# A decoder block with a mixture of experts on one core: where the gate2 rows are made, how the row of final_g comes in, and how the last scaling is cut

## The chip, the cores and the metric

The kernel runs on one NeuronCore of one Trainium2 chip, written in Bass and Tile: engines PE (matrix products), PEld (its weight loads), DVE (vector), ACT (scalar), POOL (GpSimd) and SP, which here only issues DMAs. Tile makes the semaphores and, unless a stretch of the program is marked as ordered by hand, the order of the instructions on each engine. The metric is the device time of one execution in microseconds (us).

## The reference, cut to what matters

One decoder layer on 256 tokens of 1024 numbers (float32): a mixing half (two kinds of attention, gates, output projection) and a channel half. A conditioning vector `c` gives six rows of 1024 numbers, `mod = silu(c) @ ada_w + ada_b`; the last of them is `gate2`. The half that this change touches:

```python
h2 = rmsnorm(x, norm2_g[l]) * (1.0 + scale2) + shift2
y = hierarchical_moe(h2, ...)   # top-1 of 4 groups, then top-2 of its 4 experts, SwiGLU
x = x + gate2 * y
...
return rmsnorm(x, final_g)      # x * rsqrt(mean(x*x) + eps) * final_g
```

## The kernel before

Tokens lie on partitions in two tiles of 128 (`t` = 0, 1); the 1024 columns are cut in two halves of 512 (`n` = 0, 1).

**The gate2 rows.** `adaacc[5, j]` holds, for half `j` of gate2, partial sums that lie over the partitions. `mod_rows(5)` multiplies them on PE with a square of ones, which sums over partitions and leaves the same row on all 128 of them (L477, tile `bc`, one product of 128x512 in float32, which runs as two passes each), and ACT copies the result back (L486, `adarow`). The rows are read much later, by DVE, when it weighs the down products (`weigh`, L1323). Before, `mod_rows(5)` is called in pair 0 of the experts.

**The router** (from about L1020 to L1112; order by hand on PE, DVE and ACT). The token logits lead to `rt_selb` (which experts each token takes), then PE counts positions (`rk`, L1085 to L1087), DVE makes `pos` and the one-hot tiles, and PE gathers tokens by expert (`hg`, L1212). Between these steps PE waits for DVE. In two of the waits PE does products whose result nobody reads, `keep_clock(3)` and `keep_clock(4)` (L171, tile `warm`, bf16 128x512).

**The experts.** Sixteen experts go in eight pairs `p`, two experts side by side on the 128 columns of PE's array. SP issues the loads of their weights in order through a ring of buffers: gate and up of pair `p` (`g`, `u`, L206), down of pair `p-1` (`d`, L206); for the last pair the down weights come in six pieces (L1242). PE's order is written by hand: gate products, up products (L1252), the slot weights (`st`, L1262 and L1264), the transposes of the activations (`actT`, L1286), down products (`dps`, L1309; L1297 in the last pair), and the scatter back to tokens that adds into `oacc` in PSUM (L1343), which already holds `x`. DVE weighs a down product (`yt`), ACT casts it to a high part (`yh`), DVE makes the low part (`yl`, L1330, L1335).

**The end.** `final_row` takes final_g, loaded as 8 rows of 128 numbers (`fgrow`), and spreads it on all partitions by eight small products on PE (L1138, 8 rows of the array each, two passes each) and two ACT copies (L1141, tile `fg`). It stands behind the last down products of pair 6. The columns of the last pair come in three parts (`PARTS`: 512, 256, 256). `norm_part` squares a part on ACT, with its sum per token into `ss` (L1155), and multiplies it on DVE with `fg` (L1158); `norm_end` adds the last sums (L1170), POOL takes the power −1/2 of both token tiles at once (L1171), then ACT and DVE scale (L1174, L1175, L1177), and per token tile ACT's queue issues one output transfer (L1178) and SP's another (L1179). An overflow branch behind it (more than 64 tokens for one expert) is not taken here.

Of the kernel before, what the change touches and what calls it, by code (L numbers as in the profile page):

```python
# [8 lines left out]
F32 = mybir.dt.float32  # L9
# [4 lines left out]
ALU = mybir.AluOpType  # L14
# [3 lines left out]
P = 128  # L18
D = 1024
T = 256  # L20
NT = T // P
KD = D // P
# [39 lines left out]
def hybrid_block_kernel(  # L62
# [23 lines left out]
    nc = tc.nc  # L86
    V, S, G, PE = nc.vector, nc.scalar, nc.gpsimd, nc.tensor

    x = x[0]
    out = out[0]  # L90
# [13 lines left out]
    def psa(name):  # L104
        return ps_a.tile([P, 512], F32, name=name, tag="psa")
# [61 lines left out]
    def keep_clock(n):  # L167

        ps = psa("warm").rearrange("p (b s) -> p b s", b=4)
        for _ in range(n):  # L170
            PE.matmul(ps, identb, identb.unsqueeze(1).broadcast_to([P, 4, P]), start=True, stop=True)  # L171
# [37 lines left out]
    st = Stream()  # L209
# [259 lines left out]
            V.tensor_tensor(lo, adaacc[which, j], hi.bitcast(F32), op=ALU.subtract)  # L469
            msplit[which].append((hi, lo))  # L470

    def mod_rows(which):

        for j in range(2):
            ps = psa(f"bc{which}{j}")
            if which == 5:
                PE.matmul(ps, ones, adaacc[which, j], start=True, stop=True)  # L477
            else:
                for i, part in enumerate(msplit[which][j]):
                    PE.matmul(ps, selr if (which, j) in ON_PE else onesr, part, start=(i == 0),  # L480
                              stop=(i == 1))
            if which == 4:
                V.scalar_tensor_tensor(adaacc[4, j], ps, 1.0, norm2[0][:, 512 * j:512 * j + 512],
                                       op0=ALU.add, op1=ALU.mult)
            else:
                S.copy(adaacc[which, j], ps)  # L486
# [567 lines left out]
    h2_hi(1, 1)  # L1054
    seed(1, 1)
    weigh_logits(1)
    keep_clock(3)

    larger = moe.tile([P, SETS, 16], F32, name="larger", bufs=1)
    G.memset(larger, 0.0)  # L1060
# [25 lines left out]
    PE.matmul(rk[:, NE:2 * NE], onesb, selv[:, 0, :], start=True, stop=False)  # L1086
    PE.matmul(rk[:, NE:2 * NE], strictb, selv[:, 1, :], start=False, stop=True)  # L1087
    h2_lo(0, 1)
    keep_clock(4)

    pos = keep.tile([P, NT, NE], F32, name="pos")
    V.scalar_tensor_tensor(pos, rk[:, 0:2 * NE].rearrange("p (t e) -> p t e", t=NT), 1.0, selv,
# [32 lines left out]


    PARTS = [slice(0, 512), slice(512, 768), slice(768, 1024)]
    fgrow = small.tile([P, P], F32, name="fgrow", tag="lgs")[0:KD, :]
    nc.scalar.dma_start(fgrow, final_g.rearrange("(k p) -> k p", p=P))
    fg = []  # L1130

    def final_row():

        fg.append(st.tile("fg")[:, 0:D])
        for n in range(2):
            ps = psa(f"fg{n}")
            for k in range(4):
                PE.matmul(ps[:, k * P:(k + 1) * P],  # L1138
                          ident[0:KD, 4 * n + k:4 * n + k + 1].broadcast_to([KD, P]), fgrow,
                          start=(k == 0), stop=True, skip_group_check=True)  # L1140
            S.copy(fg[0][:, 512 * n:512 * n + 512], ps)  # L1141

    norm = {}

    def norm_part(i):

        c = PARTS[i]
        n, cs = c.start // FW, slice(c.start % FW, c.start % FW + c.stop - c.start)
        if i == 0:
            norm["o"] = late.tile([P, NT, D], F32, name="o", tag="s8", bufs=2)  # L1150
            norm["ss"] = small.tile([P, len(PARTS), NT], F32, name="ssf", tag="ssf")
        o, ss = norm["o"], norm["ss"]
        for t in range(NT):
            junk = act[:, 0:c.stop - c.start]
            S.activation(junk, oacc[t][n][:, cs], AF.Square, scale=D ** -0.5,  # L1155
                         accum_out=ss[:, i, t:t + 1])
            if c is not PARTS[-1]:
                V.tensor_tensor(o[:, t, c], oacc[t][n][:, cs], fg[0][:, c], op=ALU.mult)  # L1158
        if c is not PARTS[-1]:

            if i == 0:
                V.tensor_scalar(ss[:, 0, :], ss[:, 0, :], EPS, None, op0=ALU.add)
            else:
                V.tensor_tensor(ss[:, i, :], ss[:, i, :], ss[:, i - 1, :], op=ALU.add)

    def norm_end():
        o, ss = norm["o"], norm["ss"]
        c, cs = PARTS[-1], slice(PARTS[-1].start - FW, FW)
        r = small.tile([P, NT], F32, name="rstdf", tag="rstd")
        V.tensor_tensor(r, ss[:, len(PARTS) - 1, :], ss[:, len(PARTS) - 2, :], op=ALU.add)  # L1170
        G.tensor_tensor(r, r, mhalf, op=ALU.pow)  # L1171
        for t in range(NT):
            rt_ = r[:, t:t + 1]
            S.mul(o[:, t, 0:512], o[:, t, 0:512], rt_)  # L1174
            V.scalar_tensor_tensor(o[:, t, c], oacc[t][1][:, cs], rt_, fg[0][:, c], op0=ALU.mult,  # L1175
                                   op1=ALU.mult)
            V.tensor_scalar(o[:, t, 512:c.start], o[:, t, 512:c.start], rt_, None, op0=ALU.mult)  # L1177
            nc.scalar.dma_start(out[t * P:(t + 1) * P, 0:512], o[:, t, 0:512])  # L1178
            nc.sync.dma_start(out[t * P:(t + 1) * P, 512:], o[:, t, 512:])  # L1179

    st.cycle = [ring2] * 3 + [ring] * 6 + ring1 * 3 + [ring2] + [ring3] * 2 + [ring2] * 2 + [ring]
# [174 lines left out]
    with tc.manual_schedule(engines={PE.engine}):  # L1356
        gather(0, 0)
        gather(0, 1)
        for p in range(NP):
# [15 lines left out]
            silu_up(p)  # L1375
            slot_weights(p)
            if p == 0:
                mod_rows(5)
                nmaxi = most_tokens()
                act_transpose(p)  # L1380
            else:
                down_rows(p - 1, 0)
                act_transpose(p)
                down_rows(p - 1, 1)
# [2 lines left out]
                gather((p + 1) // 2, 1)  # L1387
        p = NP - 1
        load_down(p)
        final_row()  # L1390
        scatter_pair(p - 1, 0, whole_cols[0])
        weigh_low(p - 1, 1)
        down(p, 0, PARTS[0])
# [10 lines left out]
        scatter_pair(p, 1, PARTS[2])  # L1404
        norm_part(2)

    norm_end()


    nmaxv = nc.values_load(nmaxi[0:1, 0:1], min_val=0, max_val=T)  # L1410
# [96 lines left out]
```

## Time and profile before

| | us |
|---|---|
| runs shown | 468.78, 470.38, 470.97 (median 470.38) |
| profiled execution | 470.29, its span 468.6 |
| busy in the span: PE, DVE, ACT, POOL | 448.2, 220.6, 160.6, 14.7 |
| bytes moved | 158.46 MB, 338 GB/s on the mean |
| mean granted clock of PE | 0.989 |

A busy engine need not be the bound: PE and the DMA engines are both nearly always busy while the experts run. What tells is which of them waits for the other, so the rows further down are taken from the stretches in which the change lies: the router, pair 0, the end of pair 6, and the tail.

### The profile page before, as it was taken

Reading aid. Unit: us, or ns where it says so; the run is one execution under the profiler, and the core shown is the slowest. Engines: PE = TensorE matmul, PEld = TensorE weight load, DVE = VectorE, ACT = ScalarE, POOL = GpSimd, SP = SyncE. Lnnn points to the kernel's source line nnn. Section 1 sums busy time; section 2 is a strip of 40 time slices with the busy share of each in tenths; the row PEclk is TensorE's granted clock in tenths of the full one; section 3 lists DMA queues with packets and bytes.
Section 4 is the critical chain, followed back from the end, with each engine's and each line's share of the span. In section 5 each row is a group of like instructions: output and inputs, shape, how many; then the busy total and the mean of one; then the engine's idle time right before and its main releaser. Section 6 shows DMA issues by size and latency. Waiting matters only on the chain. (4 is left out here: it accounts for less than half of the span.)

```text
span 468.6 us, 6867 instructions
## 1 busy us (share of the span) xinstructions
PE 448.2 (96%) x2724; PEld 281.2 (60%) x2724; DVE 220.6 (47%) x378; ACT 160.6 (34%) x292; POOL 14.7 (3%) x51
## 2 busy tenths in 40 slices
PE   5999999999999999999899999999999999999991
PEld 1769988976889999978453345333533335333440
DVE  5558878956999964787640030031202111020332
ACT  3543686465663444363641012011201102110222
POOL 5210000000000000000100000000000000000000
PEclk9999999999999999999999999999999999999986
DMA  8999978789797979976779999999999999999502
GB/s 290 368 324 354 295 267 287 247 287 382 254 374 255 385 263 407 422 308 219 294 258 408 424 420 418 422 419 421 420 421 419 422 419 421 420 420 404 196 0 94
DMA packets 51971, 158.46 MB, mean 338 GB/s; under 512 B 6448, under 2 KB 16728, under 8 KB 40160
## 3 DMA queue, kind: packets, MB, share of 16 engines
q1 hardware_dynamic: 51568, 157.44, 87.6%
q8 instruction: 23, 0.38, 0.3%
q10 hardware_dynamic: 368, 0.55, 0.3%
q14 instruction: 12, 0.10, 0.1%
HBM read 156.93 MB, written 1.05 MB: 337 GB/s over the span
## 5 line engine op out<-in xcount | busy, mean ns | idle before, releaser
L1252 PE MATMUL gps<-g,hg 128*64 128x512 f32 x256 | 57.9, 596 | 0.0
L1252 PE MATMUL ups<-u,hg 128*64 128x512 f32 x256 | 56.6, 595 | 0.0
L1309 PE MATMUL dps<-d,aT 128*64 128x512 f32 x224 | 51.2, 598 | 0.0
L1281 DVE TENSOR_TENSOR act<-act,ups 128x512 f32<-128x512 f32 x8 | 5.5, 687 | 93.6 <-PE ups L1252 93.6
L409 PE MATMUL g_acc<-hT,wsp 128*128 128x256 f32 x384 | 48.4, 285 | 0.3 <-DVE wsp L363 0.3
L409 PEld LDWEIGHTS g_acc<-hT,wsp 128*128 128x128 f32 x384 | 46.7, 191 | 1.6 <-issue 1.0
L1252 PEld LDWEIGHTS ups<-u,hg 128*64 128x64 f32 x256 | 17.9, 137 | 35.3 <-issue 35.3
L1252 PEld LDWEIGHTS gps<-g,hg 128*64 128x64 f32 x256 | 17.4, 137 | 33.2 <-issue 32.6
L1309 PEld LDWEIGHTS dps<-d,aT 128*64 128x64 f32 x224 | 14.8, 136 | 25.4 <-issue 25.2
L446 DVE SCALAR_TENSOR_TENSOR adarow<-adaw,cact,adarow 128x512 f32<-128x512 f32 x40 | 29.6, 743 | 0.4
L1327 ACT CAST yh<-yt 128x512 fp32r<-128x512 f32 x15 | 9.3, 618 | 56.7 <-DVE yt L1323 56.7
L1267 ACT CAST sT<-st 128x256 fp32r<-128x256 f32 x8 | 3.0, 372 | 63.4 <-PE st L1264 63.4
L940 PE MATMUL wo<-wsp,mT 128*128 128x512 f32 x96 | 23.7, 400 | 0.7 <-DVE wsp L363 0.7
L878 PE MATMUL br<-oT,wsp 128*128 128x256 f32 x192 | 23.2, 282 | 0.0
L1280 ACT ACTIVATE act<-gps 128x512 f32<-128x512 f32 x8 | 4.8, 598 | 53.7 <-PE gps L1252 53.7
L878 PEld LDWEIGHTS br<-oT,wsp 128*128 128x128 f32 x192 | 23.0, 188 | 0.2 <-DVE wsp L363 0.2
L1335 DVE TENSOR_TENSOR yl<-yt,yh 128x512 fp32r<-128x512 f32 x7 | 4.8, 692 | 34.3 <-PE oacc L1343 32.4
L940 PEld LDWEIGHTS wo<-wsp,mT 128*128 128x128 f32 x96 | 17.6, 188 | 5.2 <-DVE wsp L363 1.1
L1323 DVE SCALAR_TENSOR_TENSOR yt<-dps,ws,adarow 128x512 f32<-128x512 f32 (+1 forms) x17 | 12.2, 719 | 14.3 <-PE dps L1309 8.3
L1288 DVE COPY aT<-actT 128x512 f32<-128x512 f32 x8 | 5.5, 691 | 27.0 <-PE actT L1286 27.0
L1212 PEld LDWEIGHTS hg<-onehot,h2s 128*128 128x128 f32 x128 | 15.7, 191 | 4.2 <-ACT yh L1327 2.4
L1212 PE MATMUL hg<-onehot,h2s 128*128 128x256 f32 x128 | 16.8, 287 | 1.0 <-DVE h2s L1012 0.5
(295 smaller groups left out, 679.4 us busy)
## 6 DMA issues: line engine op xcount, KB each, us to landing
g<-in_expert_w_gate SPq DMA_DIRECT2D x32, 1024.0 KB, 14.6
u<-in_expert_w_up SPq DMA_DIRECT2D x32, 1024.0 KB, 16.3
d<-in_expert_w_down SPq DMA_DIRECT2D x30, 1024.0 KB, 17.2
adaw<-in_ada_w SPq DMA_DIRECT2D x16, 1024.0 KB, 6.4
ada<-in_ada_w SPq DMA_DIRECT2D x8, 512.0 KB, 8.9
ada<-in_ada_w SPq DMA_DIRECT2D x16, 256.0 KB, 8.5
wo<-in_w_out SPq DMA_DIRECT2D x4, 1024.0 KB, 12.9
kaw<-in_w_in SPq DMA_DIRECT2D x4, 512.0 KB, 6.6
```

What stands on the lines that cost most here:

```text
L409: PE.matmul(self.acc[m // 2][:, (m % 2) * T:(m % 2 + 1) * T], w[a][:, kk, m * P:(m + 1) * P], hT[b][:, k, :], start=(k == 0 and i == 0 and ...
L446: V.scalar_tensor_tensor(acc, adaw[which, j, k // 4][:, k % 4, :], cact[:, k:k + 1], acc, op0=ALU.mult, op1=ALU.add)
L878: PE.matmul(bacc[br][m // 2][:, (m % 2) * T:(m % 2 + 1) * T], wk[a][:, 0, m * P:(m + 1) * P], oT[br][b][:, k, :], start=(k == 0 and i == 0 ...
L940: PE.matmul(acc[t][n], mT[b][:, k, t * P:(t + 1) * P], ws[k // 2][a][:, k % 2, :], start=(k == 0 and i == 0), stop=(k == KD - 1 and i == 2))
L1212: PE.matmul(ps[:, kk * T:(kk + 1) * T], h2s[t][i][:, k * P:(k + 1) * P], oh[:, t].rearrange("p e s -> p (e s)"), start=(n == 0 and kk == 0 ...
L1252: PE.matmul(ps[64 * i:64 * i + 64, :], hg[:, k, (lo + i) * CAP:(lo + i + 1) * CAP], wt[nm, p][half][i][:, k % 4, :], start=(k == 0), stop= ...
L1280: S.activation(av, in_place(gu["g", p]), AF.Silu)
L1281: V.tensor_tensor(av, av, in_place(gu["u", p]), op=ALU.mult)
L1288: V.tensor_copy(aT, ap.rearrange("p (f s) -> p f s", f=KF))
L1309: PE.matmul(ys[p, FW * n][64 * i:64 * i + 64, :], aTs[p][:, 2 * h + k, 64 * i:64 * i + 64], dt_[p, h][i][:, k, FW * n:FW * n + FW], start= ...
L1323: V.scalar_tensor_tensor(y, ps, ws, adaacc[5, n][:, cs], op0=ALU.mult, op1=ALU.mult)
L1327: S.copy(hi, y)
```

## The change

It does four things. The gate2 rows are made one half at a time, each in the place of a `keep_clock`, in the router, and leave pair 0. `final_row` goes with its load and its ACT copies; a DMA on SP's queue, behind the last down weights, spreads final_g on all partitions. The last sum and the power are taken per token tile, in an order written by hand for DVE, ACT and POOL. And tile 0's first output transfer goes to SP's queue instead of ACT's.

```diff
@@ -469,9 +469,9 @@
             V.tensor_tensor(lo, adaacc[which, j], hi.bitcast(F32), op=ALU.subtract)
             msplit[which].append((hi, lo))
 
-    def mod_rows(which):
-
-        for j in range(2):
+    def mod_rows(which, js=(0, 1)):
+
+        for j in js:
             ps = psa(f"bc{which}{j}")
             if which == 5:
                 PE.matmul(ps, ones, adaacc[which, j], start=True, stop=True)
@@ -1054,7 +1054,7 @@
     h2_hi(1, 1)
     seed(1, 1)
     weigh_logits(1)
-    keep_clock(3)
+    mod_rows(5, (0,))
 
     larger = moe.tile([P, SETS, 16], F32, name="larger", bufs=1)
     G.memset(larger, 0.0)
@@ -1086,7 +1086,7 @@
     PE.matmul(rk[:, NE:2 * NE], onesb, selv[:, 0, :], start=True, stop=False)
     PE.matmul(rk[:, NE:2 * NE], strictb, selv[:, 1, :], start=False, stop=True)
     h2_lo(0, 1)
-    keep_clock(4)
+    mod_rows(5, (1,))
 
     pos = keep.tile([P, NT, NE], F32, name="pos")
     V.scalar_tensor_tensor(pos, rk[:, 0:2 * NE].rearrange("p (t e) -> p t e", t=NT), 1.0, selv,
@@ -1125,21 +1125,6 @@
 
 
     PARTS = [slice(0, 512), slice(512, 768), slice(768, 1024)]
-    fgrow = small.tile([P, P], F32, name="fgrow", tag="lgs")[0:KD, :]
-    nc.scalar.dma_start(fgrow, final_g.rearrange("(k p) -> k p", p=P))
-    fg = []
-
-    def final_row():
-
-        fg.append(st.tile("fg")[:, 0:D])
-        for n in range(2):
-            ps = psa(f"fg{n}")
-            for k in range(4):
-                PE.matmul(ps[:, k * P:(k + 1) * P],
-                          ident[0:KD, 4 * n + k:4 * n + k + 1].broadcast_to([KD, P]), fgrow,
-                          start=(k == 0), stop=True, skip_group_check=True)
-            S.copy(fg[0][:, 512 * n:512 * n + 512], ps)
-
     norm = {}
 
     def norm_part(i):
@@ -1155,7 +1140,7 @@
             S.activation(junk, oacc[t][n][:, cs], AF.Square, scale=D ** -0.5,
                          accum_out=ss[:, i, t:t + 1])
             if c is not PARTS[-1]:
-                V.tensor_tensor(o[:, t, c], oacc[t][n][:, cs], fg[0][:, c], op=ALU.mult)
+                V.tensor_tensor(o[:, t, c], oacc[t][n][:, cs], fg[:, c], op=ALU.mult)
         if c is not PARTS[-1]:
 
             if i == 0:
@@ -1166,16 +1151,20 @@
     def norm_end():
         o, ss = norm["o"], norm["ss"]
         c, cs = PARTS[-1], slice(PARTS[-1].start - FW, FW)
-        r = small.tile([P, NT], F32, name="rstdf", tag="rstd")
-        V.tensor_tensor(r, ss[:, len(PARTS) - 1, :], ss[:, len(PARTS) - 2, :], op=ALU.add)
-        G.tensor_tensor(r, r, mhalf, op=ALU.pow)
+        rs = small.tile([P, NT], F32, name="rstdf", tag="rstd")
+        last = len(PARTS) - 1
         for t in range(NT):
-            rt_ = r[:, t:t + 1]
-            S.mul(o[:, t, 0:512], o[:, t, 0:512], rt_)
-            V.scalar_tensor_tensor(o[:, t, c], oacc[t][1][:, cs], rt_, fg[0][:, c], op0=ALU.mult,
+            V.tensor_tensor(rs[:, t:t + 1], ss[:, last, t:t + 1], ss[:, last - 1, t:t + 1],
+                            op=ALU.add)
+        for t in range(NT):
+            G.tensor_tensor(rs[:, t:t + 1], rs[:, t:t + 1], mhalf[:, 0:1], op=ALU.pow)
+        for t in range(NT):
+            r = rs[:, t:t + 1]
+            S.mul(o[:, t, 0:512], o[:, t, 0:512], r)
+            V.scalar_tensor_tensor(o[:, t, c], oacc[t][1][:, cs], r, fg[:, c], op0=ALU.mult,
                                    op1=ALU.mult)
-            V.tensor_scalar(o[:, t, 512:c.start], o[:, t, 512:c.start], rt_, None, op0=ALU.mult)
-            nc.scalar.dma_start(out[t * P:(t + 1) * P, 0:512], o[:, t, 0:512])
+            V.tensor_scalar(o[:, t, 512:c.start], o[:, t, 512:c.start], r, None, op0=ALU.mult)
+            (nc.sync, nc.scalar)[t].dma_start(out[t * P:(t + 1) * P, 0:512], o[:, t, 0:512])
             nc.sync.dma_start(out[t * P:(t + 1) * P, 512:], o[:, t, 512:])
 
     st.cycle = [ring2] * 3 + [ring] * 6 + ring1 * 3 + [ring2] + [ring3] * 2 + [ring2] * 2 + [ring]
@@ -1375,7 +1364,6 @@
             silu_up(p)
             slot_weights(p)
             if p == 0:
-                mod_rows(5)
                 nmaxi = most_tokens()
                 act_transpose(p)
             else:
@@ -1387,7 +1375,8 @@
                 gather((p + 1) // 2, 1)
         p = NP - 1
         load_down(p)
-        final_row()
+        fg = st.tile("fg")[:, 0:D]
+        nc.sync.dma_start(fg, final_g.unsqueeze(0).broadcast_to([P, D]))
         scatter_pair(p - 1, 0, whole_cols[0])
         weigh_low(p - 1, 1)
         down(p, 0, PARTS[0])
@@ -1404,7 +1393,8 @@
         scatter_pair(p, 1, PARTS[2])
         norm_part(2)
 
-    norm_end()
+    with tc.manual_schedule(engines={V.engine, S.engine, G.engine}):
+        norm_end()
 
 
     nmaxv = nc.values_load(nmaxi[0:1, 0:1], min_val=0, max_val=T)
```

On PE, in the router, behind the start of the last `oacc` (`bc` is the product that spreads a gate2 row, `rk` the position count):

```order
 L986 MATMUL oacc_2583<-xs,ident 128x512
-L171 LDWEIGHTS identb
-L171 MATMUL warm<-identb 128x512
-L171 LDWEIGHTS identb
-L171 MATMUL warm<-identb 128x512
-L171 LDWEIGHTS identb
-L171 MATMUL warm<-identb 128x512
+L477 MATMUL bc_2586<-adarow_1597,onesr 128x512
 L1085 LDWEIGHTS strictb
 L1085 MATMUL rk<-rt_selb,strictb 128x16
```

The three unread products have gone and one `bc` stands there; the other one stands in the same way behind the third `rk` product, in place of the four.

On PE, in pair 0, from the slot weights to the gate products of pair 1, the kernel before has:

```order
L1262 MATMUL st_2741<-ident,onehot_2618 128x128 x2
L1264 MATMUL st_2741<-rt_comb,onehot_2618 128x16 x2
L477 MATMUL bc_2751<-adarow_1597,onesr 128x512
L477 MATMUL bc_2754<-adarow_1608,onesr 128x512
L1119 MATMUL pmT<-ident,rt_pmax 1x128
L1286 MATMUL actT_2765<-ident,act 128x128 x4
L1252 MATMUL gps_2796<-g_0_2772,hg 64x512
```

With the change, the same stretch of PE reads:

```order
L1251 MATMUL st_2736<-ident,onehot_2613 128x128 x2
L1253 MATMUL st_2736<-rt_comb,onehot_2613 128x16 x2
L1119 MATMUL pmT<-ident,rt_pmax 1x128
L1275 MATMUL actT_2754<-ident,act 128x128 x4
L1241 MATMUL gps_2785<-g_0_2761,hg 64x512
```

The two `bc` products are gone from between `st` and the transposes of `act`.

On DVE, in the tail, from the weighing of the middle part on, the kernel before has:

```order
L1323 SCALAR_TENSOR_TENSOR yt<-dps_3697,ws,adarow_1608 128x256
L1158 TENSOR_TENSOR o<-oacc_2533,fg 128x512
L1158 TENSOR_TENSOR o<-oacc_2567,fg 128x512
L1162 TENSOR_SCALAR ssf<-ssf 128x2
L1323 SCALAR_TENSOR_TENSOR yt<-dps_3718,ws,adarow_1608 128x256
L1158 TENSOR_TENSOR o<-oacc_2551,fg 128x256
L1158 TENSOR_TENSOR o<-oacc_2583,fg 128x256
L1164 TENSOR_TENSOR ssf<-ssf 128x2
L1170 TENSOR_TENSOR rstdf<-ssf 128x2
L1175 SCALAR_TENSOR_TENSOR o<-oacc_2551,rstdf,fg 128x256
L1177 TENSOR_SCALAR o<-o,rstdf 128x256
L1175 SCALAR_TENSOR_TENSOR o<-oacc_2583,rstdf,fg 128x256
```

With the change, from the same place on DVE:

```order
L1312 SCALAR_TENSOR_TENSOR yt<-dps_3675,ws,adarow_1608 128x256
L1147 TENSOR_SCALAR ssf<-ssf 128x2
L1143 TENSOR_TENSOR o<-oacc_2533,fg 128x512
L1143 TENSOR_TENSOR o<-oacc_2567,fg 128x512
L1312 SCALAR_TENSOR_TENSOR yt<-dps_3696,ws,adarow_1608 128x256
L1143 TENSOR_TENSOR o<-oacc_2551,fg 128x256
L1143 TENSOR_TENSOR o<-oacc_2583,fg 128x256
L1149 TENSOR_TENSOR ssf<-ssf 128x2
L1157 TENSOR_TENSOR rstdf<-ssf 128x1 x2
L1164 SCALAR_TENSOR_TENSOR o<-oacc_2551,rstdf,fg 128x256
L1166 TENSOR_SCALAR o<-o,rstdf 128x256
L1164 SCALAR_TENSOR_TENSOR o<-oacc_2583,rstdf,fg 128x256
```

`ssf`, the small sum that waits for the squares of both token tiles, has moved ahead of the two 512-wide products with `fg`, and one sum for both tiles has become two.

## Rows read from the trace of the kernel before

**Rows 1.** Windows: us, busy us (instructions) of PE, PEld, DVE, ACT, POOL, PEclk, DMA, GB/s.

```profile
226.00:241.00 15.00, 12.26 (x92) 7.45 (x92) 11.32 (x33) 9.06 (x15) 0.82 (x2) 1.00 0.95 360
241.00:441.00 200.00, 200.00 (x965) 79.25 (x961) 31.11 (x49) 26.80 (x62) 0.00 (x0) 1.00 0.99 407
441.00:450.00 9.00, 9.00 (x40) 4.34 (x39) 2.44 (x4) 1.80 (x4) 0.00 (x0) 0.81 0.00 0
```

**Rows 2.** Timeline of the router: start, us, engine, line, operation, [idle before, its releaser].

```profile
233.21 0.81 PE L171 MATMUL warm<-identb 128*128 128x512 bf16 x3
...
234.23 0.18 PE L1085 MATMUL rk<-rt_selb,strictb 128*128 128x16 bf16 x1 [0.20 <-DVE rt_selb L1080]
...
234.32 1.02 PE L171 MATMUL warm<-identb 128*128 128x512 bf16 x4
...
235.77 0.78 PE L1212 MATMUL hg<-onehot,h2s 128*128 128x256 f32 x3 [0.43 <-DVE onehot L1194]
...
238.03 0.59 ACT L1216 COPY hg<-hg 128x512 f32<-128x512 f32 x1 [4.04 <-PE hg L1212]
```

**Rows 3.** Timeline, PE and DVE in pair 0, behind the up products.

```profile
254.84 0.69 DVE L1281 TENSOR_TENSOR act<-act,ups 128x512 f32<-128x512 f32 x1 [13.53 <-PE ups L1252]
...
255.27 1.96 PE L477 MATMUL bc<-adarow,onesr 128*128 128x512 f32 x4
...
257.07 0.47 PEld L1286 LDWEIGHTS actT<-ident,act 128*128 128x128 f32 x4 [0.34 <-ACT adarow L486]
```

**Rows 4.** Loads of expert weights by line: count, issue times, us from issue to landing.

```profile
L206 SPq DMA_DIRECT2D d<-in_expert_w_down x28: 327/328/422, 225.8 to 410.2; - x28
...
DMA to landing us min/median/max: 7.1/15.5/19.9
...
L1242 SPq DMA_DIRECT2D d<-in_expert_w_down x6: 368/1209/9254, 412.7 to 432.1; - x6
...
DMA to landing us min/median/max: 10.5/15.4/20.4
```

**Rows 5.** Timeline, PE and DVE at the end of pair 6.

```profile
437.66 3.65 PE L1309 MATMUL dps<-d,aT 128*64 128x512 f32 x16
...
441.14 0.69 DVE L1330 TENSOR_TENSOR yl<-yt,yh 128x512 fp32r<-128x512 f32 x1 [0.74 <-ACT yh L1327]
...
441.25 2.05 PE L1138 MATMUL fg<-fgrow,ident 8*128 8x128 f32 x16
...
443.22 0.73 PE L1343 MATMUL oacc<-yh,sT 128*128 128x512 f32 x2
...
444.38 5.26 PE L1297 MATMUL dps<-d,aT 128*64 128x512 f32 x16
```

**Rows 6.** Windows behind the final_g products.

```profile
444.50:447.50 3.00, 3.00 (x8) 0.88 (x10) 0.69 (x1) 0.00 (x0) 0.00 (x0) 0.50 0.00 0
...
448.00:450.00 2.00, 2.00 (x10) 0.66 (x7) 0.30 (x1) 0.00 (x0) 0.00 (x0) 1.00 0.00 0
```

**Rows 7.** Timeline of the tail, and the one-column power of the router.

```profile
454.33 1.41 DVE L1158 TENSOR_TENSOR o<-oacc,fg 128x512 f32<-128x512 f32 x2 [1.13 <-ACT act L1155]
...
456.92 0.93 DVE L1158 TENSOR_TENSOR o<-oacc,fg 128x256 f32<-128x256 f32 x2 [0.67 <-ACT act L1155]
...
458.47 0.20 ACT L1155 ACTIVATION_READ_ACCUMULATOR act<-oacc 128x1 f32 x1
...
459.20 0.16 DVE L1170 TENSOR_TENSOR rstdf<-ssf 128x2 f32<-128x2 f32 x1 [1.29 <-ACT act L1155]
...
459.44 0.70 POOL L1171 TENSOR_TENSOR rstdf<-rstdf,mhalf 128x2 f32<-128x2 f32 x1 [230.29 <-DVE rstdf L1170]
...
460.18 1.33 ACT L1174 ACTIVATE o<-o,rstdf 128x512 f32<-128x512 f32 x2 [1.00 <-POOLq L1411]
...
460.95 1.01 SPq L1179 DMA_DIRECT2D out<-o  x2
...
L250 POOL TENSOR_TENSOR rstd<-rstd,mhalf x2: 557/559/561, 223.0 to 228.6; 128x1 f32<-128x1 f32 x2
```


## The prediction

> **What bounds the kernel now.** The sum below is made against the profiled execution: 470.29 us, of which the span is 468.6 and 1.69 lies around it. It stands 0.09 us under the median of the runs shown (470.38), so a change of its span carries over to the median as it is.
>
> I first cut the span into stretches by stage [rows 1]. From 241 to 441 us, where the eight pairs of experts run, PE is busy for 200.0 of 200 us, and the DMA engines are 0.99 busy too: two engines look like the bound at once. Which one it is, the landings tell [rows 4]. The last ordinary down load is issued by 410.2 and no load of that line took longer than 19.9 us, so it has landed by 430.1; PE first reads it in the second half of the down products at 437.66 [rows 5], 7.5 us later. The last pair's loads (issued from 412.7, at most 20.4 to landing) have their first user at 444.38: the first of them is there by 433.1, some 11 us ahead, and the second megabyte, issued one load later, still several. So PE waits for no weights; the loads run ahead by at least 7.5 us. **PE's own instruction stream sets the time from 241 to about 453 us**, and a us taken out of it is a us of the result as long as the sum of such cuts stays under 7.5. Behind it comes a tail in which ACT, DVE and POOL hand a last row of numbers on (453 to 462), and the transfer of the output.
>
> Ahead of it, in the router (226 to 241), PE is busy for 12.26 of 15 us only [rows 1]: it waits for DVE, twice with products that nobody reads (`warm`) in the wait [rows 2].
>
> **The change, part by part.**
>
> *1. The two gate2 products in the router.* They take the places of three and of four `warm` products [rows 2]. The three start at 233.21 and the next PE work, `rk`, at 234.23, when DVE has `rt_selb`. One gate2 product is two passes of the array. The two, four passes, stand from 255.27 on, and `actT`'s weight load, with one tiny product between, at 257.07 [rows 3]; so one is 0.90 us at most, and I take 0.88. It fits: 233.21 + 0.88 = 234.1, ahead of 234.23. The second starts at 234.32 and ends about 235.2; the gather starts at 235.77. I take 0 for both; the waits for DVE that end at 234.23 and 235.77 cover them. Were that cover gone the price would be at most 1.8 us (both products in full); below nothing it can't go, since DVE's work there is the same. ACT's two copies of the rows (0.58 us each) come behind the last `h2s` cast; ACT stands idle for 4.04 us ahead of its first `hg` copy at 238.03 [rows 2]. The gather's second buffer in PSUM now waits for such a copy, but both are done by about 236.1 (235.2, a handing over and 0.58), and the second buffer is wanted only when the first is full, which ACT copies at 238.03. Cost 0.
>
> *2. The same products taken out of pair 0.* There they stand on PE's stream, between `st` and `actT`. Without them PE would be 1.80 us earlier (255.27 to 257.07), but `actT` reads `act`, and DVE is not done with that before 254.84 + 0.69 = 255.53. With about 0.1 us for the handing over, `actT`'s weight load goes from 257.07 to about 255.62: **−1.45 us**. Bounds: −1.2 (a slower handing over, ACT's `sT` and `ws` copies in the way) and −1.8 (no wait).
>
> *3. The row of final_g.* PE's sixteen small products go: PE's step from 441.25 to 443.22, 1.97 us [rows 5]. What is late next is `yl`: DVE finishes it at 441.14 + 0.69 = 441.83, and PE, which then starts the scatter at 441.25, needs it two products later (0.58 us; the four from 443.22 to 444.38 took 1.16), at 441.83. I allow 0.1 us for that meeting: **−1.9 us** (bounds −1.6 and −2.0). In their place SP issues one load of 512 KB, the row on all 128 partitions, behind the last down loads (the last is issued at 432.1 [rows 4], now 1.5 us earlier). At the 407 GB/s of the stage [rows 1] it holds the engines for 1.3 us, behind all weights, so none of these is late. Its landing is bounded below by that transfer and above by the slowest landing of its queue, 20.4 us: 432 to 451, and I take 442 to 443, just behind the last weights, since the queue is then nearly empty. DVE asks for it at about 450. The two ACT copies that go (1.1 us at 443.4) were beside PE's work.
>
> *4. PE's clock.* At 1.00 from 226 to 441 [rows 1], the granted clock falls right behind the small products: 0.50, the 1.2 GHz level, from 444.5 to 447.5, and 1.00 (2.4 GHz) again from 448 on [rows 6]. What PE did before the fall is just the stretch with products of 8 rows instead of 128, the only such stretch among the experts. The sixteen down products behind it took 5.26 us; the same sixteen at full clock took 3.65 [rows 5]. Without the small products I expect no fall: **−1.6 us** (bounds 0, if it falls anyway, and −1.7).
>
> Against that stands a rule. The Trainium skill ("TensorE: Matmul & The Clock Gate", section "Why this matters for your kernels") puts a fall of the clock down to PE standing idle between bursts of matmuls. This case's trace does not bear that out: PE is busy for 9.00 of the 9 us from 441 to 450 [rows 1], and the clock fell all the same. By that rule the small products are not to blame, and term 4 would be 0, the sum 466.5.
>
> I keep −1.6, as the fall came right behind the one odd stretch.
>
> *5. The tail.* DVE now does the small sum `ssf` ahead of the two 512-wide products with `fg`, and `ssf` waits for both squares. DVE began these products at 454.33, between the squares; it will begin behind the second, some 0.85 us later in this stretch. That eats the 0.67 us in which DVE stood idle ahead of the next `o` at 456.92 [rows 7], and PE's last scatter waits for that one: **+0.1 us** to +0.3.
>
> Then the rstd by token tile. Tile 0's sum of squares is there at 458.47 + 0.20 = 458.67; add 0.16, the handing over 0.08, the power on one column 0.56 (against 0.70 on two) and 0.04 to ACT: ACT and DVE start tile 0 at 459.54 instead of 460.18. Tile 1's power comes behind on POOL, 459.50 to 460.06, in time for ACT's second product (half of 1.33 us later, at 460.2). So both engines end 0.64 us earlier. SP issues three transfers instead of two; it issued its two from 460.95 to 461.96, about 0.4 to 0.5 apart, so the third follows DVE's last product without a queue. With 0.1 for that: **−0.55 us** (bounds −0.2, if SP's three queue up, and −0.7).
>
> The fgrow load on ACT's queue goes; ACT works on past it. Nothing.
>
> Sum: −1.45 − 1.9 − 1.6 + 0.1 − 0.55 = −5.4 us, from 470.29 to **464.9 us**. PE's cuts ahead of the last weights' use are 1.45 + 1.9 = 3.35, under the 7.5 us by which the loads run ahead.
>
> **The rivals.**
>
> *The clock falls anyway* (chance 0.16). For it: one fall is all that the trace has, and what else may bring one is not in its rows. Against: 200 us of the experts at 1.00, and the one fall right behind the small products. The skill's rule above speaks for this rival. Then term 4 is missing, 466.5 us. A fall elsewhere, in the router, costs about the same.
>
> *PE does not gain, the loads are the bound after all* (0.05). For: DMA 0.99 busy from 241 to 441, and the lead of the loads shrinks towards the end. Against: 7.5 us are left. It decides if the lead is really near 0: terms 2 and 3 are then waits for weights, and 470.29 − 1.6 − 0.45 = 468.2 us stays.
>
> *The waits of the router are too short* (0.05): the change moves the products without getting them off the path, the gather starts 1.7 us later, 466.6 us.
>
> *Slower: the row of final_g lands late* (0.04). The one place where the change adds a wait for a transfer is DVE's first product with `fg`; behind it in DVE's queue stands the weighing of the last down part, and PE's last scatter and ACT's last squares wait for that. Each us past about 450 is a us of the result. It decides against the change past 450.2 + 5.4 = 455.6, that is over 24 us after an issue at about 431. For it: it is last in SP's queue, and 128 copies of one row are read. Against: no load of the last pair took over 20.4 us [rows 4]. At 458 it would give 464.9 + 7.8 = 472.7 us.
>
> **How the numbers follow.** The forecast has 0.70: 464.9 us. A measurement of this kernel can tell a difference of about 0.5%, here 2.35 us. The forecast, the first and the third rival are faster by more (0.91, less 0.01 for runs near the line); the second is at the line, 468.2, and counts as no change; the last is slower. That is 0.90, 0.06 and 0.04. The range reaches from 463.0 (all terms at their better bounds give −6.2, 464.1, and the runs of before differ among themselves by about a us to either side) to 467.4 (the first rival, and as much above it). It leaves out the second rival and the last, and the ends of the others.
>
> **What would show it.** In the profile after: PE's `hg` begins at about 235.8 and `gps` of pair 0 at 240.7 as before; `gps` of pair 1 begins at 256.2 to 256.4 instead of 257.7; no idle time of PE up to the scatter behind pair 6, which follows the down products without a gap at about 439.8; the clock 1.00 until the last product; sixteen `dps` products of the last pair in 3.65 us; the load of `fg` landed before 445; ACT's first scaling 0.6 us closer to the last square; the span about 463.2. It would be wrong if PE shows waits for DMA between 241 and 450, if the clock falls at the end of pair 7 without the small products, or if DVE's product with `fg` waits for a DMA.

## The result, and the profile after

| | before | after |
|---|---|---|
| median of the runs, us | 470.41 (468.78 to 470.97, 4 runs) | 464.85 (464.71 to 467.02, 4 runs) |
| profiled execution, its span, us | 470.29, 468.6 | 467.02, 465.2 |

The ratio is 0.9891, with a 95% interval of 0.9854 to 0.9928. A fifth run of after stands on record, 463.68 us, and is not in this median. One run of an experiment below, that with final_g on PE again, took 1135.12 us for a reason that nothing on record shows, and the median given there leaves it out. The predicted 464.9 us lies 0.05 us from the median; the profiled execution of after is the longest of its runs, 2.2 us above it, and the first thing to find in its trace is where those 2.2 us are. They lie near the start, in a stretch that the change does not touch. The timeline there and the windows around it (us, busy us and instructions of PE, PEld, DVE, ACT and POOL, the granted clock PEclk, DMA share, GB/s):

```profile
24.73 1.05 ACT L362 CAST wsp<-kaw 128x1024 fp32r<-128x1024 f32 x1 [4.82 <-DMA kaw<-in_w_in]
25.81 1.23 DVE L363 TENSOR_TENSOR wsp<-kaw,wsp 128x1024 fp32r<-128x1024 f32 x1 [4.64 <-ACT wsp L362]
26.96 0.69 DVE L330 COPY aacc<-ada 128x512 f32<-128x512 f32 x1
27.70 1.05 PE L336 MATMUL adat<-fold,aacc 128*128 128x1 f32 x8 [1.63 <-DVE aacc L330]
...
26.00:29.00 3.00, 1.37 (x11) 1.26 (x11) 2.99 (x6) 1.04 (x1) 0.00 (x0) 1.00 1.10 349
29.30:32.50 3.20, 3.20 (x13) 2.81 (x12) 1.69 (x5) 2.01 (x3) 0.00 (x0) 0.50 1.08 251
33.00:440.00 407.00, 403.06 (x2470) 255.16 (x2470) 192.87 (x319) 139.31 (x253) 5.13 (x27) 1.00 0.92 358
441.00:459.00 18.00, 14.06 (x74) 6.41 (x70) 8.45 (x19) 6.46 (x17) 1.06 (x2) 1.00 0.19 68
```

ACT waits for the load `kaw`; behind ACT, DVE waits to split that tile; behind the split stands the copy `aacc`, and PE waits 1.63 us for it. Then the clock is at 0.50 (1.2 GHz), and at 1.00 (2.4 GHz) from 33 to 459. In the trace of before ACT has the same load 1.25 us sooner, PE does not wait for the copy, and the clock does not fall at this place:

```profile
23.48 1.04 ACT L362 CAST wsp<-kaw 128x1024 fp32r<-128x1024 f32 x1 [2.56 <-DMA kaw<-in_w_in]
25.70 0.68 DVE L330 COPY aacc<-ada 128x512 f32<-128x512 f32 x1
26.92 0.95 PE L336 MATMUL adat<-fold,aacc 128*128 128x1 f32 x8
```

From here on after's times are compared with 2.12 us taken off, the distance of `rk` in the two traces (236.35 and 234.23).

The timeline of after, with one window in it: the router and pair 0, the end of pair 6 and the tail, for [rows 2, 3], [rows 5] and [rows 7].

```profile
235.33 1.02 PE L477 MATMUL bc<-adarow,onesr 128*128 128x512 f32 x2
236.35 0.18 PE L1085 MATMUL rk<-rt_selb,strictb 128*128 128x16 bf16 x1
...
236.45 1.10 PE L477 MATMUL bc<-adarow,onesr 128*128 128x512 f32 x2
237.89 0.51 PE L1201 MATMUL hg<-onehot,h2s 128*128 128x256 f32 x2 [0.34 <-DVE onehot L1183]
...
256.96 0.69 DVE L1270 TENSOR_TENSOR act<-act,ups 128x512 f32<-128x512 f32 x1 [13.54 <-PE ups L1241]
257.71 0.66 PE L1275 MATMUL actT<-ident,act 128*128 128x128 f32 x4
258.29 0.65 PE L1241 MATMUL gps<-g,hg 128*64 128x512 f32 x2
...
438.25 3.65 PE L1298 MATMUL dps<-d,aT 128*64 128x512 f32 x16
441.72 0.69 DVE L1319 TENSOR_TENSOR yl<-yt,yh 128x512 fp32r<-128x512 f32 x1 [0.74 <-ACT yh L1316]
441.83 0.73 PE L1332 MATMUL oacc<-yh,sT 128*128 128x512 f32 x2
442.47 0.74 PE L1332 MATMUL oacc<-yl,sT 128*128 128x512 f32 x2
443.13 3.65 PE L1286 MATMUL dps<-d,aT 128*64 128x512 f32 x16
445.00:446.00 1.00, 1.00 (x8) 0.34 (x6) 0.00 (x0) 0.00 (x0) 0.00 (x0) 1.00 0.00 0
...
452.23 1.28 DVE L1143 TENSOR_TENSOR o<-oacc,fg 128x512 f32<-128x512 f32 x2
...
456.05 1.06 POOL L1160 TENSOR_TENSOR rstdf<-rstdf,mhalf 128x1 f32<-128x1 f32 x2 [224.76 <-DVE rstdf L1157]
456.63 1.33 ACT L1163 ACTIVATE o<-o,rstdf 128x512 f32<-128x512 f32 x2 [0.35 <-POOL rstdf L1160]
```

The gate2 products end where `rk` begins, and `hg` begins 2.12 us behind before's, so they cost nothing. The transposes follow `act`, which ends at 257.65, at once. The scatter follows the down products with no products between, meets `yl` with hardly a wait, and the next sixteen `dps` take 3.65 us instead of 5.26.

PE's steps in the two traces, from the starts of the same instructions, add up:

| step on PE | before | after | difference |
|---|---|---|---|
| `rk` to `gps` of pair 1 | 23.48 | 21.94 | -1.54 |
| that to the scatter behind pair 6 | 185.51 | 183.54 | -1.97 |
| scatter to `dps` of the last pair | 1.16 | 1.30 | +0.14 |
| its sixteen `dps`, to the next scatter | 5.19 | 3.59 | -1.60 |
| that to PE's last product | 9.03 | 8.99 | -0.04 |
| PE's last product to the end | 9.99 | 9.52 | -0.47 |

That is -5.48; with the +2.12 near the start it is the -3.4 us between the two spans. (The gain in the last row of the table does not come from the output's landing: the last transfers landed 5.1 us behind their issue in before and 5.2 in after.)

### The profile page after: what moved, and what is told of

Its sections match the earlier page's. It is cut to its first block, busy times and chain, and to the rows that moved or that the text cites. A ratio compares the mean times of both kernels' runs of the same rounds, so it can differ in the third digit from the quotient of the medians.

```text
span 465.2 us, 6818 instructions
## 1 busy us (share of the span) xinstructions
PE 443.9 (95%) x2701; PEld 279.4 (60%) x2701; DVE 220.8 (47%) x379; ACT 159.6 (34%) x290; POOL 15.1 (3%) x52
## 4 chain that ended last, share of the span: by engine, by line
PE 80%; DVE 8%; DMA 6%; ACT 2%; issue 2%; SPq 1%; POOL 0%; DVEq 0%; ACTq 0%
PE gps L1241 12%; PE ups L1241 12%; PE dps L1298 11%; PE g_acc L409 7%; PE wo L940 5%; PE br L878 4%; PE oacc L1332 4%; PE hg L1201 3%; PE qb_acc L409 2%; DMA adaw<-in_ada_w 2%; PE va_acc L401 2%; PE kb_acc L409 2%; PE ka_acc L409 2%; DMA ada<-in_ada_w 2%; DVE adarow L446 2%; DMA kaw<-in_w_in 2%
```

## The experiments

Twelve kernels, in three sets; the runs of before in the three had medians of 470.41 (20 runs), 468.94 (17) and 469.01 us (18). All edits are to the changed kernel, whose 464.85 us is the measure unless another is named. No run of the changed kernel itself is in these sets; what ties them together is that the faster group of before's runs, told of below, stands at 468.5 to 469.3 us in each.

### One part undone at a time

**The gate2 rows back in pair 0**, the unread products back in the router:

```diff
-    mod_rows(5, (0,))
+    keep_clock(3)
...
-    mod_rows(5, (1,))
+    keep_clock(4)
...
             if p == 0:
+                mod_rows(5)
```

> The changed kernel with its gate2 rows back in pair 0 and the unread products back in the router's waits. My theory (the router's waits for DVE hide the rows, and PE's stream through the experts is the path): PE's gate products of pair 1 begin 1.5 us later against the gather, everything behind them too, 464.85 + 1.5 = about 466.4 us. Rival (the loads of the weights bound the experts): the 1.5 us are lost again in waits for weights, 464.9 us. Rival (the rows cost PE as much in the router as in pair 0): the gather begins up to 1.7 us earlier than in the changed kernel, and the time stays at 464.9 us.

Measured: 466.44 us (465.24 to 468.82; ratio to before 0.9929, 0.9904 to 0.9954), 1.6 us above. In its timeline the products are on PE's path again, and `gps` of pair 1 stands 1.5 us later behind `act` than in after:

```profile
254.92 0.69 DVE L1270 TENSOR_TENSOR act<-act,ups 128x512 f32<-128x512 f32 x1 [13.54 <-PE ups L1241]
255.35 1.96 PE L477 MATMUL bc<-adarow,onesr 128*128 128x512 f32 x4
257.79 0.65 PE L1241 MATMUL gps<-g,hg 128*64 128x512 f32 x2
```

(`act` to `gps` is 2.87 us here, 1.33 in after.) Terms 1 and 2 hold.

**final_g on PE again** (the definition of `final_row` and the load of `fgrow` come back with it), and **eight full-row products, sixteen passes, in that place**, with final_g by DMA:

```diff
-        nc.sync.dma_start(fg, final_g.unsqueeze(0).broadcast_to([P, D]))
+        final_row(fg)
```

> The changed kernel with the row of final_g spread by the sixteen small products on PE again, all else as changed. My theory: 1.85 us for the products, and the granted clock falls to 0.50 right behind them, 1.6 us more: 464.85 + 3.45 = about 468.3 us. Rival (the fall has nothing to do with the small products): 466.7 us, the sixteen down products of the last pair in 3.65 us. Rival (the loads bound): 464.9 us.

```diff
         nc.sync.dma_start(fg, final_g.unsqueeze(0).broadcast_to([P, D]))
+        for n in range(2):
+            ps = psa(f"full{n}")
+            for k in range(4):
+                PE.matmul(ps[:, k * P:(k + 1) * P], ident, aTs[p - 1][:, k, :],
+                          start=(k == 0), stop=True, skip_group_check=True)
```

> The changed kernel, the row of final_g still by DMA, but with sixteen unread products of the same shape and count on PE in the old place, of 128 rows instead of 8. My theory (it is the few rows that bring the clock down): the products cost their 1.9 us, and the clock stays at 1.00: 464.85 + 1.9 = about 466.8 us. Rival (any stretch of short products with a weight load each brings it down): a fall to 0.50 as in the kernel before, 468.3 us.

Measured: 467.01 us (eleven runs, 465.64 to 469.02; ratio 0.9945, 0.9924 to 0.9967) and 466.72 us (466.49 to 468.79; 0.9942, 0.9918 to 0.9967). The rows tell them apart better than the medians. With products of 8 rows:

```profile
439.87 2.05 PE L1136 MATMUL fg<-fgrow,ident 8*128 8x128 f32 x16
442.97 5.33 PE L1299 MATMUL dps<-d,aT 128*64 128x512 f32 x16
...
443.00:446.30 3.30, 3.30 (x9) 0.97 (x10) 0.69 (x1) 0.12 (x1) 0.00 (x0) 0.50 0.00 0
```

With products of 128 rows:

```profile
441.96 2.05 PE L1383 MATMUL full<-aT,ident 128*128 128x128 f32 x16
444.88 3.65 PE L1286 MATMUL dps<-d,aT 128*64 128x512 f32 x16
...
441.00:456.00 15.00, 14.63 (x86) 7.81 (x82) 6.13 (x12) 3.90 (x10) 0.00 (x0) 1.00 0.17 61
```

The same time on PE, the same place; in these two profiles the clock falls behind few rows and not behind full ones. As a fall comes in some executions only, one profile of each would be thin, but the others agree: both traces that have the 8-row products there (before and this one) have the fall behind pair 6, and none of the other twelve has it.

The median of the first lies 1.3 us below what was expected. Its single runs stand in groups, near 465.7, 466.9, 467.7 (the profiled one) and 468.9 us. Two things divide them, as far as they can be read: a fall of the clock, 1.6 to 2.1 us, in some and not in others, and some 1.2 us in the landing of the output, which the last section shows. Every profiled execution with a fall anywhere before the tail has a mean granted clock of 0.990 or less over its whole span, every one without has 0.991 or more; by that mark the runs of before divide as well: 12 of 20 stood at 470.3 or more in this set, 4 of 17 and 7 of 18 in the other two, with a mean clock of 0.988 to 0.990, and the rest at 468.5 to 469.3 with 0.991 to 0.994. Which fall a run had, the one behind pair 6 or the one near the start, the mean clock does not tell. The three runs with full rows at 468.56 to 468.79 (0.988, 0.989) are of the second kind where it can be seen: the profiled one has its fall near the start.

**The tail as before** (both powers at once, tile 0's first transfer on ACT's queue, and the order of the last step left to Tile again; two of the places that change):

```diff
-            G.tensor_tensor(rs[:, t:t + 1], rs[:, t:t + 1], mhalf[:, 0:1], op=ALU.pow)
+        G.tensor_tensor(r, r, mhalf, op=ALU.pow)
...
-            (nc.sync, nc.scalar)[t].dma_start(out[t * P:(t + 1) * P, 0:512], o[:, t, 0:512])
+            nc.scalar.dma_start(out[t * P:(t + 1) * P, 0:512], o[:, t, 0:512])
```

> The changed kernel with the last sum, the power, the scaling and the output transfers as they were before (both token tiles at once, tile 0's first transfer on ACT's queue, order left to the scheduler). My theory: the first scaling begins 0.65 us later behind the last square, and the end is 0.5 us later: 465.3 to 465.4 us. Rival (the output transfers take their time anyway, whenever the first begins): 464.9 us.

Measured: 465.65 us (465.16 to 467.63; ratio 0.9914, 0.9885 to 0.9943). From PE's last product to the end it is 9.89 us, against 9.52 in after: 0.4 us by the rows, 0.8 by the medians, whose intervals overlap. ACT's scaling begins behind one power of 0.70 us:

```profile
454.66 0.70 POOL L1156 TENSOR_TENSOR rstdf<-rstdf,mhalf 128x2 f32<-128x2 f32 x1 [225.25 <-DVE rstdf L1155]
455.40 1.33 ACT L1159 ACTIVATE o<-o,rstdf 128x512 f32<-128x512 f32 x2 [1.01 <-POOL rstdf L1156]
```

### What brings the clock down, and what PE's time is worth

**The router's waits left empty**, with the gate2 products in pair 0:

```diff
-    mod_rows(5, (0,))
...
-    mod_rows(5, (1,))
...
             if p == 0:
+                mod_rows(5)
```

> The changed kernel with the gate2 products back in pair 0 and nothing in their places in the router: no unread products, no gate2 products, PE simply waits. Theory (a wait of PE brings the granted clock down, as it seems to at 29 us): PE idles for about 1.0 and 1.5 us in a row more than now, the clock is at 0.50 for some us around 236 to 242, and the result is 466.4 (the gate2 products on the path of pair 0, as with the rows back and the unread products kept) plus 1 to 2 us: 467.5 to 468.5 where it falls. Rival (filling these waits is worth nothing): 466.4, and a clock of 1.00 from 226 to 441.

Measured: 468.46 us (466.03 to 470.8; ratio 0.9979, 0.9959 to 0.9999), 2.0 above the kernel with the unread products. PE waits 0.85 and 1.39 us, and the clock is down for nearly the whole gather:

```profile
234.39 0.18 PE L1084 MATMUL rk<-rt_selb,strictb 128*128 128x16 bf16 x1 [0.85 <-DVE rt_selb L1079]
236.01 0.98 PE L1199 MATMUL hg<-onehot,h2s 128*128 128x256 f32 x3 [1.39 <-DVE onehot L1181]
237.25 6.09 PE L1199 MATMUL hg<-onehot,h2s 128*128 128x256 f32 x29 [0.26 <-DVE h2s L1012]
...
236.00:242.50 6.50, 6.23 (x27) 5.95 (x28) 4.12 (x14) 2.95 (x5) 0.00 (x0) 0.50 0.81 297
```

So the unread products were worth their place, and the gate2 products that replace them keep the clock up as well.

**Unread products in the midst of the experts**, at the start of pair 4: eight of 8 rows, or nine dense ones, or 24 of 8 rows (this last with `aacc` moved as described below, against 465.05 us):

```diff
+            if p == 4:
+                ps = psa("tiny")
+                for k in range(8):
+                    PE.matmul(ps[:, (k % 4) * P:(k % 4 + 1) * P],
+                              ident[0:KD, k:k + 1].broadcast_to([KD, P]), aTs[p - 1][0:KD, k % 4, :],
+                              start=True, stop=True, skip_group_check=True)
```

> The changed kernel with eight unread products of 8 rows (two passes each, the form that final_row had) at the start of pair 4, in the midst of the dense experts, where PE waits for nothing. Theory (few rows bring the clock down, not waits and not the end of the program): PE loses the 1.97 us of the products, 466.8, and in part of the executions the granted clock is 0.50 for some us right behind them, another 1.6 us, 468.4; the median between the two. Rival (the fall behind pair 6 belongs to the end of the program, or to what the ACT copies or the meeting with yl do there): 466.8, and no fall in any execution.

```diff
+            if p == 4:
+                keep_clock(9)
```

> The changed kernel with nine unread bf16 products of 128x512 (about 1.94 us of PE) at the same place in pair 4. Theory (PE's stream sets the time of the experts, the loads run ahead): all of it is paid, 464.85 + 1.9 = 466.8, no fall of the clock there, and PE waits for no load. Rival (the loads set it, DMA being 0.99 busy there): less than 0.5 us is paid, 464.9 to 465.4.

(and `range(24)` in the first for the 24)

> The changed kernel with aacc's copy ahead (no fall near the start), and 24 unread products of 8 rows (two passes each, three times final_row's) at the start of pair 4. At full clock they take 5.9 us of PE's path: 465.05 + 5.9 = 470.95. Theory (products of few rows bring the clock down while PE is busy all along, and with three times as many it happens in every execution): the granted clock is 0.50 for some us in or right behind them, 472.5 to 475 in every run. Rival (the fall behind pair 6 came from something else there): 471.0 and no fall.

Measured: 466.69 us (465.69 to 468.57; ratio 0.9957, 0.9942 to 0.9973) for the eight, 466.76 us (466.73 to 467.68; 0.9955, 0.9942 to 0.9968) for the dense ones, 472.55 us (472.4 to 474.51; 1.0066, 1.0044 to 1.0089) for the 24. The dense ones are paid in full, +1.9: PE sets the time there, not the loads.

```profile
338.36 2.12 PE L171 MATMUL warm<-identb 128*128 128x512 bf16 x9
340.40 1.08 PE L1241 MATMUL gps<-g,hg 128*64 128x512 f32 x4
```

The eight settle nothing of the clock: no fall in the profile, and only one of the six runs (468.57) stands where one would be, which may as well be the fall near the start. The 24 do. Every run is 1.45 us or more above the 470.95 estimated for a clock that stays up, with a mean clock of 0.985 to 0.988, and PE was busy for 10.10 of the 10.10 us at half clock:

```profile
336.75 8.37 PE L1360 MATMUL tiny<-aT,ident 8*128 8x128 f32 x48
345.05 5.83 PE L1243 MATMUL gps<-g,hg 128*64 128x512 f32 x16
...
330.00:339.20 9.20, 9.20 (x68) 7.05 (x64) 2.19 (x3) 3.38 (x6) 0.00 (x0) 1.00 1.01 419
339.30:349.40 10.10, 10.10 (x40) 6.79 (x40) 0.00 (x0) 0.00 (x0) 0.00 (x0) 0.50 1.01 419
```

### The fall near the start

Three traces show it (after's, that with full-row products, that with nine dense products), each with `kaw` late. If DVE's order hands the lateness on to PE, one exchange in that order ends it:

```diff
+    with tc.manual_schedule(engines={PE.engine, V.engine}):
+        run("step.qa.0 hsum.1 pre.ka.1")
     with tc.manual_schedule(engines={PE.engine}):
```

(the three items leave the head of `ORDER0`; `hsum.1` is the copy `aacc`, `pre.ka.1` the split of `kaw`).

> The changed kernel with two places of DVE's order swapped near the start: the copy of a quarter's row sums (aacc) stands ahead of the split of a weight tile (kaw), not behind it, and the same for the sums that follow. In the profiles of the changed kernel and of the one with full-row products, that load landed at 24.3 and 24.5 us instead of 23.0 to 23.2 as in the four others; DVE's split started at 25.8 and 26.0 instead of 24.5, PE then waited 1.60 and 1.63 us for aacc, and the granted clock fell to 0.50 from 29.2 or 29.7 on for 3.41 us; rows behind it are 2.1 us late. Theory (a late load, through DVE's order, makes PE wait, and the wait brings the clock down): with the swap aacc waits for PE alone, PE's wait is gone even where the load is late, and with it the early fall: no execution near 467.0, all near 463.7 to 465.0, median 464.7 (before: 470.4; ratio about 0.988). Rival (the fall at 29 us has nothing to do with this wait): some executions out of 5 to 7 stay at 466.5 to 467.2, and a profile that falls on one shows the fall behind 29 us without PE's wait.

Measured: 465.05 us, and all five runs between 465.00 and 465.11 (ratio 0.9918, 0.9905 to 0.993). No run shows the fall, but five runs may have missed it, so the next two make the load late every time: the loads of `kaw` and `qaw` exchange places on SP's queue, with `aacc` behind the split and ahead of it (the first also sets the next four items of DVE's order by hand).

```diff
-... hload.1.0 hload.1.1 part.ka.1 part.qa.1 part.va.1 ...
+... hload.1.0 hload.1.1 part.qa.1 part.ka.1 part.va.1 ...
```

> The changed kernel with two neighbouring loads on SP's queue swapped, so that kaw lands behind qaw, late in every execution (24.3 us or more, where it is mostly 23.0), and the copy of aacc left behind kaw's split in DVE's order. Theory (the late load makes PE wait through DVE's order, and that wait brings the clock down): PE waits 1.6 us or more for aacc in every execution, the clock is at 0.50 for 3.41 us behind it, and the time is 467.0 (464.9 + 2.1) or a little above in all runs. Rival (the two only fell together): 465.0, with a run here and there at 467.

> The same swap of the two loads, but with the copy of aacc ahead of kaw's split in DVE's order. Theory: aacc no longer waits for the load, PE does not wait, no fall of the clock, 465.0 in every run although the load is late. Rival (a late load costs in any case, by the split or by the wait of ka's products): 466 or more.

Measured: 468.23 us (466.65 to 469.8; ratio 0.9972, 0.9952 to 0.9992) with `aacc` behind; 465.31 us (464.05 to 465.44; 0.9913, 0.9886 to 0.9939) ahead. With `aacc` behind:

```profile
26.10 1.05 ACT L362 CAST wsp<-kaw 128x1024 fp32r<-128x1024 f32 x1 [5.92 <-DMA kaw<-in_w_in]
28.32 0.68 DVE L330 COPY aacc<-ada 128x512 f32<-128x512 f32 x1
29.06 1.87 PE L336 MATMUL adat<-fold,aacc 128*128 128x1 f32 x8 [2.71 <-DVE aacc L330]
...
29.00:35.50 6.50, 6.44 (x24) 5.86 (x25) 3.76 (x10) 2.14 (x3) 1.59 (x2) 0.50 1.06 295
```

With `aacc` ahead, the load as late:

```profile
25.38 0.69 DVE L330 COPY aacc<-ada 128x512 f32<-128x512 f32 x1 [3.42 <-PE ada L325]
26.08 1.05 ACT L362 CAST wsp<-kaw 128x1024 fp32r<-128x1024 f32 x1 [5.37 <-DMA kaw<-in_w_in]
26.71 0.94 PE L336 MATMUL adat<-fold,aacc 128*128 128x1 f32 x8
...
20.00:456.00 436.00, 428.97 (x2621) 270.32 (x2619) 208.38 (x350) 150.15 (x276) 6.19 (x29) 1.00 0.90 347
```

The chain is shown: late load, split, copy, PE's wait, clock. The single runs bear it out: of the 15 runs of the three kernels with `aacc` ahead and no other products (these two sets and the version below) none has a mean clock under 0.992; of the 29 of the changed kernel and of the four above without 8-row products and with filled waits, 8 have 0.990 or less. The last link does not hold in every execution: with the load late and `aacc` behind, two of ten runs took 466.65 and 466.7 us with a mean clock of 0.993, so PE's wait alone cost about 1.8 us there, and the clock seems to have stayed up. On the median this kernel lost more than was expected (468.23 against 467.0); in its profiled run the wait was longer (2.71 us) and the clock stayed down longer (0.50 over the 6.50 us shown).

**One more version:** `aacc` ahead, and tile 0's output in one transfer.

```diff
+            if t == 0:
+                nc.sync.dma_start(out[0:P, :], o[:, 0, :])
+                continue
```

> The changed kernel with aacc's copy ahead (465.05) and token tile 0's output in one transfer of 512 KB instead of two of 256 KB, so that SP issues two transfers, not three. SP's queue holds the last transfer up by 0.3 us now: 464.8. Rival (the output's time is set by the bytes, 1 MB, or by the last transfer's own 5.2 us from issue to landing, and tile 0's first half now starts 0.4 us later): 465.0 to 465.4.

Measured: 464.21 us (463.7 to 464.91; ratio 0.989, 0.9868 to 0.9911). Against the 465.31 of the kernel just told of, from the same set but with the load late, that is 1.1 us less; against the 465.05 of the other set, from which it differs in the transfer alone, 0.8, with intervals that touch. SP issues its last transfer 0.3 us sooner behind PE's last product (2.35 us, against 2.63 with three issues), which is less than the medians differ; the rest is not explained. It is the best version measured, and its gain over the change itself lies in part in runs that no longer reach 467.

## Why the prediction was right, and where it was not

- **Router, 0 predicted, 0 measured.** `hg` begins at 237.89, that is 235.77 with the shift taken off, to the hundredth as before [rows 2].
- **Pair 0, -1.45 predicted, -1.54 by the rows, 1.6 by undoing it.** The handing over from `act` to `actT` took about 0.05 us, not 0.1.
- **final_g off PE, -1.9 predicted, -1.97 + 0.14 measured.** What is late next was `yl`, as named; the row landed well ahead: in the window from 445 to 446 no DMA moves anything, and DVE reads the row at 452.23. The rival in which it lands late is out by 7 us.
- **Clock, -1.6 predicted, -1.60 between the two traces; as a forecast of the median it held in part by luck.** The mechanism, few rows with PE busy, is shown by the 24 and by the pair of 8-row and full-row products. The rival (the clock falls anyway) is out for this place: no trace without the 8-row products has a fall behind pair 6. What the sum took wrongly is how often: it was made against one execution in which the clock fell. Against the runs of before with the higher mean clock, about 468.9 us, the change is worth 4 us (468.9 to 464.85), which is the sum without term 4 (-5.48 + 1.60). The forecast of -5.4 met a median of 470.41 that in two further sets of runs was 468.9 and 469.0. And some of before's slower runs may have had the fall near the start, which before's order of DVE allows too, and not the one behind pair 6: 23 of its 55 runs have a mean clock of 0.990 or less, but so have 8 of 29 in kernels without the 8-row products. In what share of the executions term 4 is a gain stays open.
- **Tail, +0.1 and -0.55 predicted, -0.04 and -0.47 measured.** DVE's new order took nothing from PE's last scatter. The third issue on SP's queue did queue, for about 0.3 us, where the prediction had it follow DVE without a queue; its bounds held that.
- **Loads ahead of PE.** 1.9 us more on PE's stream in pair 4 cost 1.9, and the 3.4 us of terms 2 and 3 were gained in full. How much more could be taken out before the loads bind was not tried.
- The prediction said that a fall elsewhere would cost about as much as the one behind pair 6. That happened, in the profiled execution: 2.1 us. It was put in one rival with the fall behind pair 6, although the two have different causes. The span of 463.2 us that it named is that of three other runs (462.9 to 463.1), not of the profiled one (465.2).

The prediction set its -1.6 against the rule of the Trainium skill ("TensorE: Matmul & The Clock Gate", section "Why this matters for your kernels": idle stretches between bursts lower the clock). A fall with PE busy does not speak against that rule; it shows a second cause. At two other places of this kernel the clock fell in or behind waits of PE: in the empty router (0.85 and 1.39 us, clock 0.50) and behind the late load (1.63 and 2.71 us, clock 0.50). Each of these waits is shorter than the gaps that the section warns of, so the rows agree with it in kind only.

## What to carry to other kernels

A profile is one execution: before a stall in it is booked as a gain, look whether the runs stand in groups, because a stall that only some executions have is worth only its share. Fill the waits of PE with products that are needed anyway and use all rows; products of a few rows cost their time and can cost the clock behind them. Where an engine works in order, put what another engine waits for ahead of what waits for a load, even if the load is nearly always in time.

## What the runs showed that was not expected

- Products of 8 rows lower the clock with PE never idle: 0.50 over 10.10 busy us in and behind 24 of them and over 3.30 behind the eight of final_g, against 1.00 behind eight products with 128 rows in the same place. Eight of them brought the fall in some executions and not in others; what decides that was not settled.
- One load, `kaw`, with the same loads ahead of it, ended ACT's wait at 23.3 to 23.6 us in nine traces and at 24.7 to 24.9 in the three with the fall near the start; no run tells why.
- The last output transfers of 256 KB on SP's queue landed 5.1 or 5.2 us behind their issue in five traces of the same form, after's among them, and 3.9 to 4.2 in six, which moves the end by about 1 us:

```profile
out<-o SPq DMA_DIRECT2D x3, 256.0 KB, 5.2
```

is the row of DMA issues of after (count, size, median us to landing), and that of the kernel with the late load and `aacc` ahead is

```profile
out<-o SPq DMA_DIRECT2D x3, 256.0 KB, 3.9
```

That kernel took 465.3 to 465.4 us in three runs and 464.05 in the profiled one, to which this row belongs.
